# A two-layer DiT kernel on one core: which engine forms six of the 24 modulation units, and where in the program

## The chip, the core and the metric

The kernel runs on one core of a Trainium2 chip. Its engines run side by side, each in its own order: TensorE (PE; its weight loads are listed as PEld), VectorE (DVE), ScalarE (ACT), GpSimd (POOL), and SyncE (SP), which here issues DMAs. They wait for each other by semaphores. The metric is the device time of one execution in microseconds (us), the median of the runs taken; lower is better.

## The reference, cut to what matters

Two layers over 512 latent rows and 256 context rows, width 2048, in float32. Each layer first forms a modulation (shift, scale, gate) for both kinds of rows from two condition vectors:

```python
for i in range(DEPTH):                                  # DEPTH = 2
    shift, scale, gate       = split((silu(c)     @ ada_w[i] + ada_b[i])[:, None, :], 3)   # 2048 -> 3*2048
    shift_c, scale_c, gate_c = split( silu(c_ctx) @ ada_w[i] + ada_b[i], 3)
    h  = rmsnorm(x,  norm_w[i]) * (1 + scale)   + shift
    hc = rmsnorm(xc, norm_w[i]) * (1 + scale_c) + shift_c
    y, yc = even_mix(h, hc, ...) if i % 2 == 0 else odd_mix(h, hc, ...)   # both begin with h @ w_in, hc @ w_in
    x = x + gate * y
    if need_ctx: xc = xc + gate_c * yc                  # layer 0 only
return rmsnorm(x, final_norm)
```

`even_mix` (layer 0) is pooling and latent attention; `odd_mix` (layer 1) is a bidirectional mLSTM and windowed attention.

## The kernel before, in words

The modulation weights are two matrices of 2048 x 6144, together 24 **units** of 2048 x 512 (4 MB each). Units 0 to 7 are the shift and scale of layer 0, 8 to 11 its gate, 12 to 19 the shift and scale of layer 1, 20 to 23 its gate. A unit is needed for both condition vectors, except 20 to 23, which the context rows don't use: these are the **light** units here, the others the **heavy** ones. There are three ways to form a unit:

- `ada_steps` (L133), units 0 to 7 at the start: PE multiplies in float32, 16 matmuls of 32 columns of weights into the four quarters of one PSUM tile `pa`.
- `ada_pe_steps` (L154), units 18 and 19: the same, in four batches of four matmuls; DVE transposes the result (`gat`, L167), PE folds it (`pb`, L170) and DVE adds the bias (`av`, L131).
- `ada_vec_steps` (L174), the other 14 units: no PE. A step loads 256 KB of weights (`at`, L180, a DMA from SP into one of four buffers) and DVE multiplies it by a scalar and adds it to an accumulator (`acc`, L187): two such instructions in a heavy step, one in a light one. After 16 steps each accumulator is transposed and reduced (`atr`, `red`, L192 and L193: two more steps in a heavy unit, one in a light one), and one fold on PE (`pb`, L199) with four `av` on DVE ends the unit.

`Background` (L206) takes such steps one by one; `bg.step(n)` lets the surrounding code put n of them at a place.

The **in-projection** of layer 0 is 14 groups of 256 columns. Its groups 2 to 13 are `in_group` (L502): for each of four quarters `kq`, `load_w` (L111) loads 512 KB of weights (`wraw`, three buffers) and splits them in two **halves** into a rounded part (`wh`, a cast on ACT, L108) and a rest (`wl`, a subtraction on DVE, L109), four buffers each; then `tmode` (L301) multiplies: 24 pairs of a 512-row matmul into `px` (L309) and a 256-row one into `pc` (L311) per quarter. Groups 4 to 7 also do the pooling: `pool_mean` on DVE, then `pool_mix`, six short matmuls (`ppx`, L568) after quarters 1 and 3 of groups 5 and 7. Behind group 13 comes latent attention.

The **value products** of layer 1 are `mv_group` (L1199), heads 1 to 3: `kmode` (L314, matmuls at L322) with `load_w` in the same way, and between them `ctx_state` (L1215), which scales the context's values on DVE (`wv`, L1219), splits them (`wvh` on ACT, `wvl` on DVE) and multiplies them on PE (L1228). One more group of the same width follows (`odw[5]`, L1239).

PE's order in these stages, and all other engines', comes from a scheduler that places each instruction by its own estimate; so a step can stand some way off from where the code puts it. Each engine then works strictly in that order, and SP too: a `wraw` load behind an `at` load is not issued before it.

Of the kernel before, what the change touches and what calls it, by code (L numbers as in the profile page):

```python
# [8 lines left out]
F32 = mybir.dt.float32  # L9
# [7 lines left out]
P = 128  # L17
# [21 lines left out]
def tile_hybrid_dit(ctx: ExitStack, tc: tile.TileContext, ts: dict, out: bass.AP, dbg=None, upto=99):  # L39
    nc = tc.nc  # L40
    T, V, S, G, DM = nc.tensor, nc.vector, nc.scalar, nc.gpsimd, nc.sync

    def opool(es, name, side=None, bufs=1):
        return es.enter_context(tc.tile_pool(name=name, bufs=bufs, side=side, reuse_waits="tile"))
# [16 lines left out]
    def ppool(es, name, **bufs):  # L61
        return Banks(es, name, **bufs)
# [24 lines left out]
    st = cst.tile([P, KC, 32], F32, name="st")  # L87
# [12 lines left out]
    fold = con[:, C_FOLD : C_FOLD + 32]  # L100
# [24 lines left out]
    def ada_place(u, pb, n):  # L125

        a = cst.tile([P, 4, 2], F32, name=f"av{u}")
        for b4 in range(4):
            sl = slice(32 * b4, 32 * b4 + 32)
            ab = vec[sl, V_AB + 8 * u : V_AB + 8 * u + 8].rearrange("p (b v) -> p b v", v=2)  # L130
            V.tensor_tensor(a[sl, :, :n], pb[:, :n, b4::4].rearrange("p v b -> p b v"), ab[:, :, :n], op=ALU.add)  # L131
        av[u] = a

    def ada_steps(u, pp, tp, nb=3, nt=2):

        pa = pp.tile([P, 512], F32, name=f"pa{u}", tag="pm")
        for q in range(4):
            at = []
            for i in range(2):
                at.append(tp.tile([P, 2, 512], F32, name=f"at{u}_{q}_{i}", tag="ada", bufs=nb))  # L140
                DM.dma_start(at[i], ts["ada"][u, 2 * q + i].rearrange("p (k w) -> p k w", w=512))
            for qd in range(4):
                T.matmul(pa[32 * qd : 32 * qd + 32, :], st[:, 4 * q + qd, :], at[qd // 2][:, qd % 2, :],
                         start=q == 0, stop=q == 3, skip_group_check=True)
            if q == 3:
                tr = tp.tile([P, 16, 32], F32, name=f"ga{u}", tag="ga", bufs=1)
                V.transpose(tr.rearrange("p b r -> p (b r)"), pa)
                yield
                pb = pp.tile([32, 2, 16], F32, name=f"pb{u}", tag="pm")
                T.matmul(pb, fold, tr[:, :, 0:2].rearrange("p b v -> p v b"), start=True, stop=True)  # L150
                ada_place(u, pb, 2)
            yield

    def ada_pe_steps(u, pp, tp, nb):  # L154

        pa = pp.tile([P, 512], F32, name=f"pa{u}", tag="pm")
        for q in range(4):
            at = []
            for i in range(4):
                kc = 4 * q + i  # L160
                at.append(tp.tile([P, 512], F32, name=f"at{u}_{kc}", tag="ada", bufs=nb))
                DM.dma_start(at[i], ts["ada"][u, kc // 2][:, (kc % 2) * 512 : (kc % 2) * 512 + 512])
            for qd in range(4):
                T.matmul(pa[32 * qd : 32 * qd + 32, :], st[:, 4 * q + qd, :], at[qd], start=q == 0, stop=q == 3, skip_group_check=True)
            if q == 3:
                tr = ta("gat", 512).rearrange("p (b r) -> p b r", r=32)
                V.transpose(tr.rearrange("p b r -> p (b r)"), pa)  # L167
                yield
                pb = pp.tile([32, 2, 16], F32, name=f"pb{u}", tag="pm")
                T.matmul(pb, fold, tr[:, :, 0:2].rearrange("p b v -> p v b"), start=True, stop=True)  # L170
                ada_place(u, pb, 2)
            yield
# [183 lines left out]
    pp = ppool(esP, "ppA", px=4, pc=2, pm0=1, pm1=1)  # L356

    def new_px(n=1):
        return [pp.tile([P, 512], F32, name="px", tag="px", bufs=4) for _ in range(n)]

    def new_pc():
        return pp.tile([P, 2, 256], F32, name="pc", tag="pc", bufs=2)
# [94 lines left out]
    ap_ = opool(esA, "phA")  # L457
    OX, OC, NP = 8, 8 + NX + 8, 8 + NX + 8 + NC + 8

    def ta(name, n=NT):  # L460
        return ap_.tile([P, NP], F32, name=name, tag="ta", bufs=6)[:, :n]

    def c_evac(pairs, ssq):

        res = []
        for px, pc in pairs:
            r = ta("craw")
            S.copy(r[:, :NX], px)
            V.tensor_copy(r[:, NX:], pc)
            res.append(r)  # L470
        for r in res:
            sq = ta("csq") if ssq[1] else ssq[0]
            S.activation(sq, r, AF.Square)
            if ssq[1]:
                V.tensor_tensor(ssq[0], ssq[0], sq, op=ALU.add)
            ssq[1] += 1
        return res
# [12 lines left out]
    pc = new_pc()  # L490
# [9 lines left out]
    S.copy(kr[:, NX:], pc[:, 0, :])  # L500
    split(kr, KH, KL)

    bg = Background(range(8, 14), pp, ap_, 4, "ta", 6)

    def in_group(g, between=(), steps=(1, 1)):
        px, pc = new_px(2), new_pc()
        for kq in range(4):
            w = load_w(win[g, kq])
            bg.step(steps[0])
            tmode(px, [pc[:, b, :] for b in range(2)], w, range(4 * kq, 4 * kq + 4), HX0, HC0, kq == 0, kq == 3)  # L510
            bg.step(steps[1])
            if kq < len(between):
                between[kq]()
        return px, pc
# [2 lines left out]
    ssq = [ap_.tile([P, NT], F32, name="ssqc", tag="ssqc", bufs=1), 0]  # L517
    raw = []
    for g in range(2):
        px, pc = in_group(2 + g, steps=(2, 2))  # L520
        raw += c_evac([(px[b], pc[:, b, :]) for b in range(2)], ssq)
    p6 = pp.tile([P, 6], F32, name="cps6", tag="pm")
    stat_mm(p6, ssq[0], 6, 512)
# [46 lines left out]
        return z  # L570

    for pr in range(2):
        px, pc = in_group(4 + 2 * pr, steps=(1, 0))
        ds, zs = [], []

        def mean(b):
            ds.append(pool_mean(2 * pr + b, px[b], pc[:, b, :]))

        def mix(b):
            zs.append(pool_mix(2 * pr + b, ds[b]))  # L580

        mean(0)
        qx, qc = in_group(5 + 2 * pr, (lambda: mean(1), lambda: mix(0), lambda: None, lambda: mix(1)), (0, 0))
        for b in range(2):
            t = ta("psg")
            S.activation(t[:, :NX], qx[b], AF.Silu)
            S.activation(t[:, NX:], qc[:, b, :], AF.Silu)
            V.tensor_tensor(t, zs[b], t, op=ALU.mult)
            G.dma_start(zd[2 * pr + b], t)


    for i in range(6):
        if i < 2:
            pe = ada_pe_steps(18 + i, pp, ap_, 4)
            px, pc = in_group(8 + i, (lambda: next(pe), lambda: next(pe), lambda: next(pe), lambda: (next(pe), next(pe))), (0, 0))
        else:
            px, pc = in_group(8 + i, steps=(2, 2))
        for b in range(2):
            t = ta("sag")
            S.activation(t[:, :NX], px[b], AF.Silu)  # L600
            S.activation(t[:, NX:], pc[:, b, :], AF.Silu)
            G.dma_start(agd[2 * i + b], t)
# [7 lines left out]
    pp = ppool(esP, "ppM", s2=2, pj=2, pm=2)  # L610
# [19 lines left out]
    for j in range(4):  # L630
        r = tf("cqr")
# [276 lines left out]
    pp = ppool(esP, "ppO", px=4, pc=2, pm=2)  # L908
# [3 lines left out]
    bg = Background(range(14, 18), pp, tz, 4, "ht", 3)  # L912
# [66 lines left out]
    for i in range(2):  # L979
        for b, px in enumerate(x_group_t(G_MQ + i)):  # L980
            q = htp.tile([P, NX], F32, name="mqt", tag="mqt", bufs=2)
# [54 lines left out]
    for i in range(2):  # L1036
        px, pc = new_px(2), new_pc()
# [98 lines left out]
    for d in range(2):  # L1136
# [20 lines left out]
        tr = gs.tile([4, 4], F32, name="tr", tag="tr", bufs=2)  # L1157
# [34 lines left out]
    eg.close()  # L1192


    ea = ExitStack()
    bg = Background(range(20, 24), pp, opool(ea, "ada1"), 4, "atr", 1)


    def mv_group(h, state):  # L1199
        px, pc = new_px(2), new_pc()  # L1200
        pv = [px[b // 2][:, 256 * (b % 2) : 256 * (b % 2) + 256] for b in range(4)]
        for kq in range(4):
            w = load_w(odw[1 + h, kq])
            kcs = range(4 * kq, 4 * kq + 4)
            bg.step(2)
            kmode(pv, w, kcs, HX, kq == 0, kq == 3, 2)
            bg.step(3)
            kmode([pc[:, b, :] for b in range(2)], w, kcs, HC, kq == 0, kq == 3, 2)
            if kq % 2 == 0:
                next(state, None)  # L1210
        vx_store(h, [p_.rearrange("p (a b) -> p a b", b=256) for p_ in px])
        return vc_store([pc])
# [25 lines left out]
    px, pc = new_px(2), new_pc()  # L1238
    for kq in range(4):  # L1239
        w = load_w(odw[5, kq])  # L1240
        bg.step(2)
        tmode(px, [pc[:, b, :] for b in range(2)], w, range(4 * kq, 4 * kq + 4), HX, HC, kq == 0, kq == 3)
        if kq % 2 == 0:
            next(state, None)
    bg.finish()
    ea.close()
    for b in range(2):
        t = cm.tile([P, NX], F32, name="akx", tag="kxt", bufs=2)
        S.copy(t, px[b])
# [24 lines left out]
    pp = ppool(esP, "ppL", px=4, pm=4)  # L1274
# [168 lines left out]
    pp = ppool(esP, "ppW", px=2, s2=2, pm=1, po=1)  # L1443
# [303 lines left out]
    pp = ppool(esP, "ppF", px=4, pm=2)  # L1747
    for g in range(3, 7):
        px = new_px(2)
# [13 lines left out]
    for h in range(2):  # L1763
        sl = slice(256 * h, 256 * h + 256)
        px = [p_[:, :256] for p_ in new_px(2)]
# [138 lines left out]
```

## Time and profile before

| | |
|---|---|
| median of 3 runs | 2305.13 us (2303.32 to 2306.37) |
| the profiled execution, its own time | 2305.76 us |
| its span | 2304.0 us |
| PE, PEld busy | 2229.1 us (97%), 1894.9 us (82%) |
| DVE, ACT, POOL busy | 1406.7 us (61%), 916.3 us (40%), 162.8 us (7%) |
| in-projection groups 2 to 13 | about 164 to 589 us of the span |
| value products and the group behind them | about 1412 to 1570 us |

In the profile an instruction is named by line, engine, operation and tile, as `L187 DVE ... acc<-at,st,acc`. A matmul's listed duration overlaps with the next one's; the time that a matmul takes is read from the distance of two starts.

### The profile page before, as it was taken

How to read it: one execution, taken by the hardware profiler on the slowest of the kernel's cores; microseconds unless marked ns; L12 is line 12 of the kernel's file. 1: busy time of each engine (PE TensorE's matmuls, PEld its weight loads, DVE VectorE, ACT ScalarE, POOL GpSimd, SP SyncE). 2: the span in 40 equal slices, each digit the busy share in tenths (PEclk: the TensorE clock that was granted, in tenths of full speed). 3: DMA queues.
4: the chain of work that ended last, by engine and by line, in shares of the span. 5: the costliest groups of instructions: out<-in, count | busy, mean ns of one | idle time of the engine just before them, and what ended most of it. 6: DMA issues, size and time to landing. Idle time of an engine off the chain costs nothing. (4 is left out here: it accounts for less than half of the span.)

```text
span 2304.0 us, 34221 instructions
## 1 busy us (share of the span) xinstructions
PE 2229.1 (97%) x13000; PEld 1894.9 (82%) x13000; DVE 1406.7 (61%) x2841; ACT 916.3 (40%) x1864; POOL 162.8 (7%) x203
## 2 busy tenths in 40 slices
PE   5999999999999999999999999999999999999998
PEld 3678888788899999888888799988888878777887
DVE  5579523296666666788558524763455587778434
ACT  4232222112444444542226322223556667656432
POOL 0000100000000000011113100000000000003110
PEclk9999999999999999999999999999999999999999
DMA  9855323565211112276444321753232312113433
GB/s 386 322 202 179 121 85 115 185 227 186 100 49 54 51 56 69 101 252 224 160 158 154 93 100 65 247 185 120 88 101 94 103 61 68 65 55 122 135 113 116
DMA packets 118005, 309.14 MB, mean 134 GB/s; under 512 B 13612, under 2 KB 21292, under 8 KB 117840
## 3 DMA queue, kind: packets, MB, share of 16 engines
q1 hardware_dynamic: 110960, 279.64, 36.2%
q0 software_dynamic: 6880, 27.32, 3.2%
q8 instruction: 102, 1.67, 0.3%
q14 instruction: 63, 0.52, 0.1%
HBM read 277.28 MB, written 29.62 MB: 133 GB/s over the span
## 5 line engine op out<-in xcount | busy, mean ns | idle before, releaser
L108 ACT CAST wh<-wraw 128x512 fp32r<-128x512 f32 (+2 forms) x540 | 316.1, 590 | 852.5 <-PE pc L311 372.1
L109 DVE TENSOR_TENSOR wl<-wraw,wh 128x512 fp32r<-128x512 f32 (+2 forms) x540 | 358.5, 669 | 467.7 <-ACT wh L108 464.4
L187 DVE SCALAR_TENSOR_TENSOR acc<-at,st,acc 128x512 f32<-128x512 f32 x360 | 251.9, 749 | 25.8 <-DMA at<-in_ada_dram 24.2
L322 PE MATMUL px<-wh,hxh 128*128 128x512 f32 (+2 forms) x512 | 174.9, 342 | 0.8 <-ACT sz L1310 0.8
L322 PE MATMUL px<-wl,hxh 128*128 128x512 f32 (+2 forms) x512 | 174.0, 340 | 0.0
L322 PE MATMUL px<-wh,hxl 128*128 128x512 f32 (+2 forms) x512 | 173.9, 340 | 0.0
L309 PE MATMUL px<-h0h,wh 128*128 128x512 f32 x384 | 152.9, 398 | 0.0
L309 PE MATMUL px<-h0h,wl 128*128 128x512 f32 x384 | 151.7, 395 | 0.3 <-DVE wl L109 0.3
L309 PE MATMUL px<-h0l,wh 128*128 128x512 f32 x384 | 151.6, 395 | 0.0
L311 PE MATMUL pc<-h0h,wl 128*128 128x256 f32 x400 | 112.7, 282 | 0.0
L311 PE MATMUL pc<-h0h,wh 128*128 128x256 f32 x400 | 112.5, 281 | 0.0
L311 PE MATMUL pc<-h0l,wh 128*128 128x256 f32 x400 | 112.4, 281 | 0.0
L322 PEld LDWEIGHTS px<-wh,hxh 128*128 128x128 f32 x512 | 96.7, 189 | 13.6 <-ACT sz L1310 1.9
L322 PEld LDWEIGHTS px<-wl,hxh 128*128 128x128 f32 x512 | 96.7, 189 | 11.2
L322 PEld LDWEIGHTS px<-wh,hxl 128*128 128x128 f32 x512 | 96.6, 189 | 11.2
L309 PEld LDWEIGHTS px<-h0h,wh 128*128 128x128 f32 x384 | 72.1, 188 | 22.9 <-ACT wh L108 4.2
L309 PE MATMUL px<-hxh,wh 128*128 128x512 f32 x224 | 89.7, 400 | 0.0
L309 PE MATMUL px<-zxl,wh 128*128 128x512 f32 x224 | 89.3, 399 | 0.0
L309 PE MATMUL px<-hxl,wh 128*128 128x512 f32 x224 | 89.2, 398 | 0.0
L309 PE MATMUL px<-hxh,wl 128*128 128x512 f32 x224 | 89.1, 398 | 0.0
L309 PE MATMUL px<-zxh,wl 128*128 128x512 f32 x224 | 88.7, 396 | 0.0
L309 PE MATMUL px<-zxh,wh 128*128 128x512 f32 x224 | 88.2, 394 | 0.0
(887 smaller groups left out, 6010.1 us busy)
## 6 DMA issues: line engine op xcount, KB each, us to landing
at<-in_ada_dram SPq DMA_DIRECT2D x256, 256.0 KB, 3.4
at<-in_ada_dram SPq DMA_DIRECT2D x64, 512.0 KB, 7.9
wraw<-in_od_in_dram SPq DMA_DIRECT2D x64, 512.0 KB, 3.5
wraw<-in_ev_in_dram SPq DMA_DIRECT2D x56, 512.0 KB, 4.2
wraw<-in_ev_out_dram SPq DMA_DIRECT2D x44, 512.0 KB, 3.9
wraw<-in_od_oz_dram SPq DMA_DIRECT2D x32, 512.0 KB, 3.5
wraw<-in_od_out_dram SPq DMA_DIRECT2D x32, 512.0 KB, 3.5
xt<-in_xT_dram SPq DMA_DIRECT2D x16, 384.0 KB, 7.3
```

The source lines that it names most:

```text
L108: S.copy(h, src)
L109: low.tensor_tensor(l, src, h, op=ALU.subtract)
L187: V.scalar_tensor_tensor(a, at, st[:, kc, v : v + 1], a, op0=ALU.mult, op1=ALU.add)
L309: T.matmul(px[b], w_, Hx[kc][r_], start=s0, stop=s1)
L311: T.matmul(pc[b], w_, Hc[kc][r_], start=s0 and b == 0, stop=s1, skip_group_check=True)
L322: T.matmul(p_, h_, w_, start=s0, stop=s1, skip_group_check=True)
```

## The change

Units 18 and 19 leave PE, and `ada_pe_steps` is removed; units 20 to 23 leave the value products; all six become steps of `ada_vec_steps` under the in-projection. Its list of units grows from six to twelve: 8, 9, then the light 20 to 23, then 10 to 13, 18 and 19. The steps per quarter change from 2+2, 1+0, 0+0 and 2+2 in groups 2-3, 4 and 6, 5 and 7 to 9, and 10-13, to 2+1 in groups 2-3, 2+2 in groups 4 to 7, and 3+2 in groups 8 to 13.

```diff
-    def ada_pe_steps(u, pp, tp, nb):
...
-    bg = Background(range(8, 14), pp, ap_, 4, "ta", 6)
+    bg = Background((8, 9, 20, 21, 22, 23, 10, 11, 12, 13, 18, 19), pp, ap_, 4, "ta", 6)
...
-        px, pc = in_group(2 + g, steps=(2, 2))
+        px, pc = in_group(2 + g, steps=(2, 1))
...
-        px, pc = in_group(4 + 2 * pr, steps=(1, 0))
+        px, pc = in_group(4 + 2 * pr, steps=(2, 2))
...
-        qx, qc = in_group(5 + 2 * pr, (lambda: mean(1), lambda: mix(0), lambda: None, lambda: mix(1)), (0, 0))
+        qx, qc = in_group(5 + 2 * pr, (lambda: mean(1), lambda: mix(0), lambda: None, lambda: mix(1)), (2, 2))
...
     for i in range(6):
-        if i < 2:
-            pe = ada_pe_steps(18 + i, pp, ap_, 4)
-            px, pc = in_group(8 + i, (lambda: next(pe), lambda: next(pe), lambda: next(pe), lambda: (next(pe), next(pe))), (0, 0))
-        else:
-            px, pc = in_group(8 + i, steps=(2, 2))
+        px, pc = in_group(8 + i, steps=(3, 2))
...
-    ea = ExitStack()
-    bg = Background(range(20, 24), pp, opool(ea, "ada1"), 4, "atr", 1)
...
-            bg.step(2)
             kmode(pv, w, kcs, HX, kq == 0, kq == 3, 2)
-            bg.step(3)
             kmode([pc[:, b, :] for b in range(2)], w, kcs, HC, kq == 0, kq == 3, 2)
...
-        bg.step(2)
         tmode(px, [pc[:, b, :] for b in range(2)], w, range(4 * kq, 4 * kq + 4), HX, HC, kq == 0, kq == 3)
...
-    bg.finish()
-    ea.close()
```

On PE, at the end of quarter 0 of group 8, the first batch of unit 18 stands between two pairs before:

```order
L309 MATMUL px<-h0h_167,wl 128x512
L311 MATMUL pc<-h0h_167,wl 128x256
L164 MATMUL pa_3408<-at_0_3409,st 32x512
L164 MATMUL pa_3408<-at_1_3411,st 32x512
L164 MATMUL pa_3408<-at_2_3413,st 32x512
L164 MATMUL pa_3408<-at_3_3415,st 32x512
L309 MATMUL px<-h0h_169,wh 128x512
L311 MATMUL pc<-h0h_169,wh 128x256
```

There are eight such batches in groups 8 and 9; now the pairs follow each other without them, and in groups 8 to 13 only six folds of two short matmuls (`pb<-red`) stand between pairs.

On DVE, groups 8 and 9 before (L588 is the end of the pooling, `gat` and `av` belong to units 18 and 19, `acc` in the last row to unit 10):

```order
L588 TENSOR_TENSOR psg<-pz,psg 128x768 x2
L109 TENSOR_TENSOR wl<-wraw,wh 128x512 x8
L167 STREAM_TRANSPOSE gat<-pa_3408 128x512
L131 TENSOR_TENSOR av_3635<-pb_3633,vec 32x8 x4
L109 TENSOR_TENSOR wl<-wraw,wh 128x512 x8
L167 STREAM_TRANSPOSE gat<-pa_3709 128x512
L131 TENSOR_TENSOR av_3936<-pb_3934,vec 32x8 x4
L187 SCALAR_TENSOR_TENSOR acc_0_2788<-at_4_3962,st,acc_0_2788 128x512
```

and in the changed program a stretch of the same groups (L167 is now the line of the accumulation, here of unit 10):

```order
L109 TENSOR_TENSOR wl<-wraw,wh 128x512
L167 SCALAR_TENSOR_TENSOR acc_0_3756<-at_4_3843,st,acc_0_3756 128x512
L167 SCALAR_TENSOR_TENSOR acc_1_3757<-at_5_3847,st,acc_1_3757 128x512
L167 SCALAR_TENSOR_TENSOR acc_0_3756<-at_5_3847,st,acc_0_3756 128x512
L167 SCALAR_TENSOR_TENSOR acc_1_3757<-at_6_3851,st,acc_1_3757 128x512
L167 SCALAR_TENSOR_TENSOR acc_0_3756<-at_6_3851,st,acc_0_3756 128x512
L109 TENSOR_TENSOR wl<-wraw,wh 128x512
```

Where a half's split `wl` stood next to the next one, five or six accumulations stand between them now; this goes on to the end of group 13.

On DVE in the value products, around the scaling `wv` of head 2's context state before (`acc` is unit 22):

```order
L187 SCALAR_TENSOR_TENSOR acc_0_15034<-at_5_15141,st,acc_0_15034 128x512
L109 TENSOR_TENSOR wl<-wraw,wh 128x512
L187 SCALAR_TENSOR_TENSOR acc_0_15034<-at_6_15196,st,acc_0_15034 128x512
L187 SCALAR_TENSOR_TENSOR acc_0_15034<-at_7_15199,st,acc_0_15034 128x512
L1219 TENSOR_SCALAR wv<-vcx,wcol 128x258 x2
L187 SCALAR_TENSOR_TENSOR acc_0_15034<-at_8_15250,st,acc_0_15034 128x512
L109 TENSOR_TENSOR wl<-wraw,wh 128x512
L109 TENSOR_TENSOR wvl<-wv,wvh 128x516
```

and now, for the same head (`wv` is L1190, `c0l` the rest of the state formed before):

```order
L109 TENSOR_TENSOR wl<-wraw,wh 128x512 x4
L109 TENSOR_TENSOR c0l_13447<-pc_15226,c0h_13446 128x258
L109 TENSOR_TENSOR wl<-wraw,wh 128x512
L1190 TENSOR_SCALAR wv<-vcx,wcol 128x258 x2
L109 TENSOR_TENSOR wl<-wraw,wh 128x512
L109 TENSOR_TENSOR wvl<-wv,wvh 128x516
```

No accumulation, and so no wait for an `at` load, stands ahead of `wv` any more. Outside these two stages the order of every engine is as before.

## Rows read from the trace of the kernel before

**Rows 1.** Waits of PE, whole span: total us, times, longest.
```profile
PE ps L267 <- DVE rb L395: 23.0, 1, 23.0
...
PE pc L1228 <- ACT wvh L108: 3.9, 1, 3.9
...
PE px L309 <- DVE wl L109: 0.3, 1, 0.3
```
**Rows 2.** Timeline of PE in group 8: start, us, instruction.
```profile
384.86 0.39 PE L309 MATMUL px<-h0h,wl 128*128 128x512 f32 x1
...
385.29 1.07 PE L164 MATMUL pa<-at,st 128*32 128x512 f32 x8
386.29 0.50 PE L309 MATMUL px<-h0h,wh 128*128 128x512 f32 x1
...
386.75 0.40 PE L309 MATMUL px<-h0l,wh 128*128 128x512 f32 x1
```
**Rows 3.** The same: quarters 24 pairs apart, starts of groups 8, 10, last pair, fold.
```profile
254.47 0.40 PE L309 MATMUL px<-h0h,wh 128*128 128x512 f32 x1
...
262.95 0.40 PE L309 MATMUL px<-h0h,wh 128*128 128x512 f32 x1
...
376.74 0.39 PE L309 MATMUL px<-h0h,wh 128*128 128x512 f32 x1
...
479.17 0.39 PE L309 MATMUL px<-h0h,wl 128*128 128x512 f32 x1
...
479.79 0.50 PE L309 MATMUL px<-h0h,wh 128*128 128x512 f32 x1
...
496.54 0.39 PE L309 MATMUL px<-h0h,wh 128*128 128x512 f32 x1
...
504.86 0.39 PE L309 MATMUL px<-h0h,wh 128*128 128x512 f32 x1
...
588.47 0.39 PE L309 MATMUL px<-h0h,wl 128*128 128x512 f32 x1
```
**Rows 4.** Stretches: us, busy us per engine (x), PE's granted clock, DMA share, GB/s.
```profile
1480.00:1490.00 10.00, 10.00 (x88) 10.00 (x87) 6.72 (x14) 3.42 (x6) 0.54 (x1) 1.00 0.76 253
1490.00:1500.00 10.00, 8.97 (x77) 8.77 (x76) 5.47 (x9) 1.10 (x2) 0.00 (x0) 1.00 0.71 237
1500.00:1510.00 10.00, 6.26 (x38) 6.06 (x39) 8.18 (x16) 2.66 (x5) 0.00 (x0) 0.83 0.87 283
```
**Rows 5.** Timeline of all engines there: start, us, instruction, idle before it.
```profile
1498.09 1.54 DVE L187 SCALAR_TENSOR_TENSOR acc<-at,st,acc 128x512 f32<-128x512 f32 x2 [3.83 <-DMA at<-in_ada_dram]
...
1501.59 0.61 DVE L1219 TENSOR_SCALAR wv<-vcx,wcol 128x258 f32<-128x258 f32 x2
...
1502.91 0.38 PE L1228 MATMUL pc<-wvh,mkch 128*128 128x258 f32 x1 [3.94 <-ACT wvh L108]
```
**Rows 6.** Timeline of DVE in groups 10 and 11.
```profile
464.62 5.39 DVE L187 SCALAR_TENSOR_TENSOR acc<-at,st,acc 128x512 f32<-128x512 f32 x8 [1.76 <-DMA at<-in_ada_dram]
469.93 1.29 DVE L109 TENSOR_TENSOR wl<-wraw,wh 128x512 fp32r<-128x512 f32 x2
471.13 5.39 DVE L187 SCALAR_TENSOR_TENSOR acc<-at,st,acc 128x512 f32<-128x512 f32 x8
...
477.64 1.30 DVE L192 STREAM_TRANSPOSE atr<-acc 128x512 f32<-128x512 f32 x2
478.86 1.24 DVE L193 TENSOR_REDUCE red<-atr 128x16 f32<-128x512 f32 x2
480.01 0.48 DVE L182 TENSOR_SCALAR acc<-at,st 128x512 f32<-128x512 f32 x1
```
**Rows 7.** Timeline of DVE later in group 12.
```profile
539.02 0.69 DVE L109 TENSOR_TENSOR wl<-wraw,wh 128x512 fp32r<-128x512 f32 x1 [3.47 <-ACT wh L108]
```
**Rows 8.** DVE by line, 164 to 589 us: busy us, mean ns, idle before.
```profile
L187 DVE SCALAR_TENSOR_TENSOR acc<-at,st,acc 128x512 f32<-128x512 f32 x174 | 118.6, 744 | 4.3 <-DMA at<-in_ada_dram 4.1
```
**Rows 9.** The same, 1412 to 1570 us.
```profile
L187 DVE SCALAR_TENSOR_TENSOR acc<-at,st,acc 128x512 f32<-128x512 f32 x60 | 44.9, 749 | 18.5 <-DMA at<-in_ada_dram 17.2 <-DVE acc L187 0.3
```

More of the change, by code (lines that the diff above doesn't have):

```diff
@@ L146, in ada_steps @@
                 tr = tp.tile([P, 16, 32], F32, name=f"ga{u}", tag="ga", bufs=1)
[L147 to L152, printed above, removed]
-    def ada_pe_steps(u, pp, tp, nb):
[L156 to L166, printed above, removed]
                 V.transpose(tr.rearrange("p b r -> p (b r)"), pa)
```

## The prediction

> **What bounds the kernel now.** I read the page first: PE is busy 97% of the span, so a change pays only if it takes work or a wait off PE. Then the waits of PE [rows 1]: the largest, 23.0 us, lies at the start and is not touched; of the two stages that are, the value products have one wait of 3.9 us for `wvh`, and the whole in-projection has 0.3 us. So the in-projection is bound by PE's own work, which the timeline measures [rows 2, 3], and the value products lose time at one place, which the stretches and the timeline of all engines show [rows 4, 5]. The reader is to see in rows 2 that a batch of `pa` pushes two pairs apart, in rows 4 that two stretches hold fewer matmuls than the one before. The question is then whether DVE can carry six more units under the in-projection without making PE wait; that is read from DVE's timeline and its groups by line [rows 6 to 9].
>
> **In-projection, PE.** A pair normally starts 0.35 us after the one before. Around a batch of four `pa` matmuls the distance is 386.29 - 384.86 = 1.43 us, and the next pair takes 0.46 us [rows 2]; so a batch costs 1.43 + 0.46 - 2 x 0.35 = 1.19 us, and the eight that go cost 9.5 us.
>
> Not all of that need come back, because pairs run at two paces: 24 of them, a quarter, took 8.48 us at 254 us and 8.32 us at 497 us [rows 3], with PE waiting for nothing at either place. Groups 8 to 13 took from 376.74 to 588.47 + 0.35, 212.1 us. In the changed order they hold 24 quarters and six folds. A fold costs 0.62 - 0.35 = 0.27 us in its own distance (479.17 to 479.79) and, by the pair behind the batch, 0.11 us more: 0.38 us. At the slow pace that is 24 x 8.48 + 6 x 0.38 = 205.8 us, a gain of 6.3 us; at the fast pace 202.0 us, a gain of 10.1 us. I take the slow one: group 8 is entered slow before, and the pace changed there only behind longer interruptions (pooling, `pa`), which groups 8 to 13 no longer have, while the fold at 479 left a fast pace fast. Both ends stay in the range.
>
> Folds elsewhere: groups 2 to 7 get five instead of one (units 8, 9, 20, 21, 22), 1.5 us more; the value products and the group behind them lose the four of units 20 to 23, for which I use the same price, 1.5 us less. They cancel.
>
> **Value products.** Stretches of 10 us hold 88 matmuls, then 77, then 38 [rows 4]: 61 are missing, at 10 / 88 = 0.114 us each 6.9 us. [...] The cause stands in rows 5: DVE sat 3.83 us before an accumulation until its `at` load had come, `wv` was queued behind that accumulation and started at 1501.59, and PE's matmul followed at 1502.91. With no accumulation ahead of `wv` the stall goes with its slow clock: 6.9 us. What is late next there: `wv` waits for ACT's copy of the values at a group's end, and PE wants `wvh` a quarter later, 72 matmuls or 8.2 us, while `wv` to the matmul took 1.3 us. So nothing takes its place; the lower bound is no gain, if ACT's copy or cast is the late one.
>
> **In-projection, DVE: what the six units cost and what hides them.** Eight accumulations took 5.31 us (464.62 to 469.93), 0.664 us each; two splits 1.20 us; two transposes 1.22 us, two reductions 1.15 us; a first product is 0.48 us [rows 6]. With four bias adds, bounded by a reduction (0.6 us), a heavy unit is 30 x 0.664 + 0.5 + 1.2 + 1.2 + 0.6 = 23.4 us in 18 steps, 1.30 us a step. At five steps a quarter in groups 9 to 13, DVE needs 6.5 + 1.2 = 7.7 us against PE's 8.3 to 8.5 us: 92%, dense but enough. In groups 4 to 7 a light step is one accumulation, and the pooling has room.
>
> The cover is the lead. A half may be split as soon as PE leaves the fourth half before it; at 539.02 a split had waited 3.47 us for just that [rows 7], so DVE was ahead by nearly three halves, 3 x 4.2 us less a cast and a split, about 11 us. And with eight accumulations between splits [rows 6], denser than the five or six now, PE waited only 0.3 us in the stage. If the cover went, each us that DVE is behind a quarter would be a us of PE in each of 20 quarters.
>
> The loads: four buffers reach four steps ahead. For heavy steps that is 8 x 0.664 = 5.3 us, and in the in-projection 174 accumulations (87 loads) waited 4.1 us, 0.05 us a load [rows 8]. For light steps it is 2.7 us, and 60 accumulations waited 17.2 us, 0.29 us each [rows 9]. So units 20 to 23 bring such waits into groups 4 to 8: four steps and two splits are 4 x (0.664 + 0.29) + 1.2 = 5.0 us of a quarter's 8.48. Volume: five loads of 256 KB and one of 512 KB in 8.48 us are about 216 GB/s, while one stretch moved 283 GB/s [rows 4]. Free, then, with this end kept: if heavy loads also waited 0.29 us, a quarter would be 7.7 + 1.45 = 9.15 us, PE would fall behind by 20 x (9.15 - 8.48) - 11 = 2.4 us.
>
> [...]
>
> **Sum.** 6.3 + 6.9 = 13.2 us off. The profiled execution took 2305.76 us (span 2304.0), 0.03% from the median, so the median moves alike: 2305.1 - 13.2 = 2292 us.
>
> **Rivals.**
> 1. *The fast pace*: groups 8 to 13 at 8.32 us a quarter give 10.1 + 6.9 = 17.0 us, 2288 us. For it: the late groups run fast before. Against: what turned them fast is taken out.
> 2. *DVE is just too slow, or the stall in the value products only shrinks*: waits of 0.29 us a heavy load, or a late cast there. The gain is then 13.2 less 2.4 to 6.9 us: 2294 to 2299 us. For it: light loads did wait so long. Against: rows 8, and the short chain of rows 5.
> 3. *The loads pace DVE, and DVE paces PE; slower*. SP issues in order, so a weight load stands behind loads that wait for DVE, and a late load delays the split behind it, the next load's buffer, and the weights. With w us of waiting a load, PE loses 20 x (7.7 + 5w - 8.48) - 11 us. That eats the 13.2 us at w = 0.40; at w = 0.5 it is 23 us, 2315 us, and each pause of PE adds a slow clock as in rows 4. For it: the 0.29 us of rows 9 and the 216 GB/s of loads, all through one queue. Against: 0.05 us in rows 8.
> 4. *Nothing measurable*: w about 0.35, or a new stall at the change to attention, where DVE carries four leftover steps (as before, but from a shorter lead): 2301 to 2309 us.
>
> **Chances.** Main 0.48, rival 1 0.25, rival 2 0.14, rival 4 0.08, rival 3 0.05. The range from 2285 to 2300 us holds the first three, with 3 us below rival 1 for both terms' error. What this kernel's measurement can tell from no change is about 0.2%, 4.6 us; below 2300.5 us counts as faster: 0.48 + 0.25 + 0.14 = 0.87, within 0.08, slower 0.05.
>
> **What would show it.** In the changed profile: no `pa` after 150 us, and groups 8 to 13 in 202 to 206 us; a quarter of 8.48 or 8.32 us settles the pace. DVE's splits there still waiting for ACT now and then, as in rows 7; PE's wait for `wl` under 1 us. In the value products no wait for `wvh`, every 10 us stretch at 86 to 88 matmuls and a clock of 1.00. I am wrong if `px` waits for `wl` by several us, if `acc` waits for `at` by over 0.3 us a load in groups 9 to 13, or if the wait for `wvh` stays.

## The result, and the profile after

| | before | after |
|---|---|---|
| median | 2305.81 us, 6 runs (2303.32 to 2309.93) | 2293.77 us, 6 runs (2288.86 to 2296.03) |
| ratio | | 0.9942, 95% interval 0.9927 to 0.9957 |
| profiled execution, span | 2305.76, 2304.0 us | 2295.59, 2293.8 us |
| DVE busy | 1406.7 us (61%) | 1452.3 us (63%) |

The kernel became 12.0 us faster; 13.2 us were forecast (2292 us, range 2285 to 2300). Where the profiled executions part is read from when PE reaches the same instruction in each:

| PE reaches | before | after | difference, us |
|---|---|---|---|
| the first `gkr` matmul, early in the in-projection | 50.25 | 52.04 | +1.8 |
| group 8, first pair | 376.74 | 379.04 | +2.3 |
| group 13, last pair | 588.47 | 584.34 | -4.1 |
| `pc<-wvh`, the last ahead of the old stall | 1481.28 | 1477.39 | -3.9 |
| `pc<-wvh`, the first behind its slow clock | 1523.58 | 1512.46 | -11.1 |
| `pc<-wvh`, the last of the stage | 1558.70 | 1547.41 | -11.3 |
| `bc`, in the next stage | 1575.60 | 1565.30 | -10.3 |

Groups 8 to 13 gained 6.4 us and the stretch with the stall 7.2 us, both where the prediction put them. Of the 7.2 us, 0.4 belong to a fold (`pb`) of a light unit that stood there before:

```profile
1511.80 0.28 PE L322 MATMUL px<-wh,hxl 128*128 128x256 f32 x1
1512.01 0.23 PE L199 MATMUL pb<-red,con 128*32 128x16 f32 x2
1512.17 0.38 PE L322 MATMUL pc<-wh,hch 128*128 128x256 f32 x1
1512.39 0.28 PE L322 MATMUL pc<-wl,hch 128*128 128x256 f32 x1
```

The matmuls around it take 1512.39 - 1511.80 = 0.59 us where two take 0.23 elsewhere. So the stall itself gave back 6.8 us.

The 1.8 us at the start are hardly from the change. The stretch from 45 to 50 us shows what they are; its columns are those of [rows 4], with all engines. Before:

```profile
45.00:50.00 5.00, 5.00 (x27) 3.40 (x27) 0.67 (x2) 0.07 (x1) 0.00 (x0) 0.85 1.02 411
```

After:

```profile
45.00:50.00 5.00, 5.00 (x19) 2.61 (x18) 1.02 (x2) 0.42 (x1) 0.00 (x0) 0.50 1.02 410
```

Behind the same early pause of 2.15 us PE runs at a granted clock of 0.50 for the whole 5 us in this execution; in the other it is 0.50 up to 46.5 us and 1.00 from 47 us on. In the profiles of the experiments, which share this opening, the same instruction comes from 1.5 us earlier to 1.8 us later than before; it is 1.4 us later in one that leaves the kernel before as it was up to there (heavy_only_six) and 0.3 us later in one that has the whole change (toggle). A single profile can be off by that much. The one of the changed kernel lies 1.8 us above the median of its runs, the one before at its median, which fits the 12.0 us of the medians against the 10.2 us of the spans.

The timeline of PE after, which answers to [rows 2, 3]: the first pairs of two quarters of group 8, the pair ahead of a fold and the one behind it, and the last pair of group 13.

```profile
379.04 0.39 PE L289 MATMUL px<-h0h,wh 128*128 128x512 f32 x1
...
387.51 0.40 PE L289 MATMUL px<-h0h,wh 128*128 128x512 f32 x1
...
404.12 0.39 PE L289 MATMUL px<-h0h,wl 128*128 128x512 f32 x1
...
404.72 0.50 PE L289 MATMUL px<-h0h,wh 128*128 128x512 f32 x1
...
584.34 0.39 PE L289 MATMUL px<-h0h,wl 128*128 128x512 f32 x1
```

A quarter takes 387.51 - 379.04 = 8.47 us, the slow pace, and a fold 0.60 us between pairs. The six groups take 584.34 + 0.35 - 379.04 = 205.65 us; forecast were 205.8 us.

The three stretches with the same times as in [rows 4]:

```profile
1480.00:1490.00 10.00, 10.00 (x88) 10.00 (x87) 3.08 (x7) 3.53 (x6) 0.54 (x1) 1.00 0.33 112
1490.00:1500.00 10.00, 10.00 (x88) 10.00 (x87) 2.48 (x5) 2.14 (x4) 0.00 (x0) 1.00 0.29 97
1500.00:1510.00 10.00, 10.00 (x88) 10.00 (x87) 1.39 (x2) 1.24 (x2) 0.00 (x0) 1.00 0.17 54
```

88 matmuls in each, clock 1.00: no pause and no slow clock behind it. Before, the clock was 0.50 from about 1504 to 1507 us, behind the pause, and 1.00 from 1508 us on. Of PE's waits, those of the value products and the steps behind them, 1412 to 1600 us (total us, times, longest), this is the only one:

```profile
PE bc L1304 <- ACT selh L1256: 1.1, 1, 1.1
```

It wasn't there before, and in this profile about 1 us of what the stage gave back (-11.3 to -10.3 in the table) is lost again at the next hand-over. ACT had itself waited 1.1 us for a load (`selr`) that was issued 6.3 us earlier; before, 4.5 us lay between the two and nobody waited. In light_only, toggle and double_mix below, which have lost the stall too, PE doesn't wait there. So this wait is not shown to be a price of the change.

DVE under the in-projection, answering to [rows 6, 7]: one stretch at the end of group 9, one in group 12.

```profile
443.83 0.69 DVE L109 TENSOR_TENSOR wl<-wraw,wh 128x512 fp32r<-128x512 f32 x1 [2.15 <-ACT wh L108]
448.07 0.69 DVE L109 TENSOR_TENSOR wl<-wraw,wh 128x512 fp32r<-128x512 f32 x1 [3.55 <-ACT wh L108]
...
526.54 3.40 DVE L167 SCALAR_TENSOR_TENSOR acc<-at,st,acc 128x512 f32<-128x512 f32 x5
529.85 0.68 DVE L109 TENSOR_TENSOR wl<-wraw,wh 128x512 fp32r<-128x512 f32 x1
530.46 3.39 DVE L167 SCALAR_TENSOR_TENSOR acc<-at,st,acc 128x512 f32<-128x512 f32 x5
534.01 0.69 DVE L109 TENSOR_TENSOR wl<-wraw,wh 128x512 fp32r<-128x512 f32 x1 [0.16 <-ACT wh L108]
```

DVE still waits now and then for the buffers that PE has to leave (3.55 us, and 0.16 in the densest part, behind casts of ACT of which those at 443 and 533 us had themselves waited 3.6 us for PE), so its lead is full again there; five accumulations cost 529.85 - 526.54 = 3.31 us, 0.662 each. Its groups by line over groups 8 to 13 (379 to 585 us), answering to [rows 8], and over groups 4 to 7 (246 to 379 us):

```profile
L167 DVE SCALAR_TENSOR_TENSOR acc<-at,st,acc 128x512 f32<-128x512 f32 x183 | 125.4, 743 | 3.8 <-DMA at<-in_ada_dram 3.4
...
L167 DVE SCALAR_TENSOR_TENSOR acc<-at,st,acc 128x512 f32<-128x512 f32 x58 | 43.6, 751 | 18.2 <-DMA at<-in_ada_dram 16.9
```

The light units took their waits along, 16.9 / 58 = 0.29 us a load, as in the value products [rows 9]; the heavy ones waited 3.4 us over 183 accumulations. In neither place did PE notice: it waits for no `wl` in groups 2 to 13.

### The profile page after: what moved, and what is told of

Same layout as the page of the kernel before. It is cut to its first block, busy times and chain, and to the rows that moved or that the text cites. A ratio compares the mean times of both kernels' runs of the same rounds, so it can differ in the third digit from the quotient of the medians.

```text
span 2293.8 us, 34183 instructions
## 1 busy us (share of the span) xinstructions
PE 2220.6 (97%) x12936; PEld 1892.2 (82%) x12936; DVE 1452.3 (63%) x2909; ACT 918.4 (40%) x1866; POOL 163.8 (7%) x203
## 5 line engine op out<-in xcount | busy, mean ns | idle before, releaser
L167 DVE SCALAR_TENSOR_TENSOR acc<-at,st,acc 128x512 f32<-128x512 f32 x420 | 294.1, 749 | 24.6 <-DMA at<-in_ada_dram 22.9
L289 PEld LDWEIGHTS px<-h0h,wl 128*128 128x128 f32 x384 | 72.1, 188 | 17.6
```

The lines of the kernel that those rows point to most:

```text
L167: V.scalar_tensor_tensor(a, at, st[:, kc, v : v + 1], a, op0=ALU.mult, op1=ALU.add)
L289: T.matmul(px[b], w_, Hx[kc][r_], start=s0, stop=s1)
```

## The experiments

Each is compared with the kernel before, run beside it on the same chip. The changed kernel was not run beside them: where one is set against it, about 1 us stays open, since the kernel before has medians from 2304.63 to 2305.81 us in the sets.

**The light units alone.** The changed kernel's list without 18 and 19; these stay on PE as before.

```diff
-    bg = Background(range(8, 14), pp, ap_, 4, "ta", 6)
+    bg = Background((8, 9, 20, 21, 22, 23, 10, 11, 12, 13), pp, ap_, 4, "ta", 6)
...
-        px, pc = in_group(4 + 2 * pr, steps=(1, 0))
+        px, pc = in_group(4 + 2 * pr, steps=(2, 2))
...
-            px, pc = in_group(8 + i, steps=(2, 2))
+            px, pc = in_group(8 + i, steps=(3, 2))
```

(Groups 5 and 7 get 2+2 steps too, and the value products lose theirs, as in the change.)

> Only the light units 20 to 23 move under the in-projection (2+2 steps in groups 2 to 7, 3+2 in groups 10 to 13); units 18 and 19 stay on PE in groups 8 and 9. Theory, two separate gains: the value products lose their stall (7.1 us between the two traces), groups 8 to 13 keep their 212 us, and the folds in groups 2 to 7 cost about 0.5 us: 2305.8 - 7.1 + 0.5 = about 2299 us, no wait for wvh. Rival, one gain that needs both parts (the units on PE also kept DVE's order or PE's pace from what the changed kernel has): either no gain beyond 2 us, or nearly the whole 12 us.

2299.67 us, ratio 0.9977 (0.9967 to 0.9988). PE's waits hold no `wvh`; groups 8 to 13 took 591.39 + 0.35 - 378.64 = 213.1 us, 1 us over before.

**The heavy units alone.**

```diff
-    bg = Background(range(8, 14), pp, ap_, 4, "ta", 6)
+    bg = Background((8, 9, 10, 11, 12, 13, 18, 19), pp, ap_, 4, "ta", 6)
...
-        px, pc = in_group(4 + 2 * pr, steps=(1, 0))
+        px, pc = in_group(4 + 2 * pr, steps=(2, 0))
...
-        if i < 2:
-            pe = ada_pe_steps(18 + i, pp, ap_, 4)
...
+        px, pc = in_group(8 + i, steps=(2, 2))
```

> Only units 18 and 19 leave PE, to DVE under the in-projection (2+2 steps in groups 8 to 13, 2+0 in groups 4 and 6); units 20 to 23 stay in the value products. Theory, two separate gains: groups 8 to 13 fall from 212 us to 205.6 us at the slow pace of 8.48 us a quarter, the wait for wvh stays near 3.9 us: 2305.8 - 6.5 = about 2299 us. Should groups 8 to 13 run at 8.32 us a quarter, 2295 us. Rival: the gain of groups 8 to 13 is not the pa batches but comes with the lighter DVE queue elsewhere: then less than 3 us.

2299.14 us, ratio 0.9970 (0.9957 to 0.9982). Groups 8 to 13 took 581.16 + 0.35 - 375.84 = 205.7 us, and the wait in the value products is still there (PE's waits):

```profile
PE pc L1224 <- ACT wvh L108: 3.1, 1, 3.1
```

The two parts gain 5.4 and 6.0 us, 11.4 together, and both at once 12.0: they are separate, each in its own stage, as the sum had them.

**Six buffers in the value products.** What late thing made the stall?

```diff
-    bg = Background(range(20, 24), pp, opool(ea, "ada1"), 4, "atr", 1)
+    bg = Background(range(20, 24), pp, opool(ea, "ada1"), 6, "atr", 1)
```

> The kernel before, with six at buffers instead of four for the units in the value products; nothing else. Theory A, the stall there comes from loads that are issued too late (four buffers reach only 2.7 us ahead, a load takes 3.4 to 3.6 us): with six, 4 us ahead, DVE's 17 us of waiting for at shrink to under 6 us and the wait for wvh to under 1 us: about 2299 us. Theory B, the load is held behind a weight load or by the sharing of the DMA engines, whatever its buffer: the wait for wvh stays at 3 to 4 us, 2304 to 2306 us.

2300.13 us, ratio 0.9972 (0.9961 to 0.9984). Theory A. PE's waits in the value products, DVE by line from 1412 to 1570 us, and the stretch that had held 38 matmuls:

```profile
PE pc L1228 <- DVE wvl L109: 0.4, 1, 0.4
```

```profile
L187 DVE SCALAR_TENSOR_TENSOR acc<-at,st,acc 128x512 f32<-128x512 f32 x60 | 45.0, 749 | 5.7 <-DMA at<-in_ada_dram 4.4
```

```profile
1500.00:1510.00 10.00, 10.00 (x87) 9.84 (x86) 9.72 (x16) 1.25 (x2) 0.00 (x0) 1.00 0.91 287
```

The wait for `wvh` is gone, 17.2 us of waiting for loads [rows 9] became 4.4, and the 38 matmuls 87, with all 60 accumulations still in place and DVE busy 97% of that stretch. So DVE was not too full there; its loads were asked for too late.

**Both at once, the other way.** Units 18 and 19 to DVE, six buffers in the value products, the light units left where they were: the two edits above, joined.

> Units 18 and 19 leave PE for DVE, units 20 to 23 stay in the value products with six at buffers there. Theory, the two gains add and the stall needs only the earlier loads: 2305 - 6 (as with the heavy units alone) - 5 to 7 (as with six buffers alone) = 2292 to 2294 us, level with the changed kernel. Rival, moving the light units gives something that earlier loads do not: 2296 us or more, with a wait of PE for wvh or wvl left over 1 us.

2293.56 us, ratio 0.9947 (0.9934 to 0.9960): level with the changed kernel.

```profile
PE pc L1224 <- DVE wvl L109: 0.8, 1, 0.8
...
PE pc L1224 <- ACT wvh L108: 0.3, 1, 0.3
```

PE still waits these 1.1 us there, but moving the light units gives nothing on top that can be measured.

**Two buffers under the in-projection.** Is the cover that the prediction named the real one?

```diff
-    bg = Background((8, 9, 20, 21, 22, 23, 10, 11, 12, 13, 18, 19), pp, ap_, 4, "ta", 6)
+    bg = Background((8, 9, 20, 21, 22, 23, 10, 11, 12, 13, 18, 19), pp, ap_, 2, "ta", 6)
```

> The changed kernel with two at buffers instead of four under the in-projection. Theory, four buffers are what hides the loads: two reach two heavy steps ahead, 2 x 1.33 = 2.7 us, under the 3.4 us to landing and the issue; each heavy load waits 0.5 to 0.75 us, and the formula of the third rival, 20 x (7.7 + 5w - 8.48) - 11, gives 23 to 48 us: 2317 to 2342 us, with px or pc waiting for wl. Rival, the loads are not near the limit: DVE waits more for at, but PE loses less than 3 us, 2297 us at most.

2348.31 us, ratio 1.0190 (1.0174 to 1.0205): 54 us slower than the changed kernel, over the range. DVE from 379 to 600 us, then PE's waits from 164 to 700 us (in part), and the first pair of group 8 and the last of group 13:

```profile
L167 DVE SCALAR_TENSOR_TENSOR acc<-at,st,acc 128x512 f32<-128x512 f32 x162 | 114.5, 748 | 57.1 <-DMA at<-in_ada_dram 56.2
```

```profile
PE pj L642 <- DVE av L131: 14.2, 1, 14.2
PE pj L642 <- DVE vl L109: 8.7, 1, 8.7
PE px L289 <- DVE wl L109: 8.4, 7, 1.9
PE cps L247 <- DVE ssqc L455: 5.5, 1, 5.5
```

```profile
391.73 0.39 PE L289 MATMUL px<-h0h,wh 128*128 128x512 f32 x1
...
612.55 0.40 PE L289 MATMUL px<-h0h,wl 128*128 128x512 f32 x1
```

81 loads waited 56.2 us, 0.69 each; the formula gives 20 x (7.7 + 3.5 - 8.48) - 11 = 43 us. The last pair of group 13 comes 612.55 - 584.34 = 28 us later. But group 8 already starts 391.73 - 379.04 = 12.7 us later: ahead of it PE waits 5.5 us for `ssqc`, a sum of squares that DVE reaches late among its accumulations, and has a clock of 0.50 from 245 to 250 us. Groups 8 to 13 themselves lose 15.5 us. Then the attention stands 14.2 us and 8.7 us, because DVE has steps left over, and PE's clock is 0.67 from 620 to 640 us. From group 8 on the loss is some 42 us (54 less 12.7), near the formula's 43; but most of it is paid in the attention, where DVE settles what it still owes, and the 12.7 us ahead of the dense groups are not in the formula.

**Denser steps.** How much room was left?

```diff
-        px, pc = in_group(8 + i, steps=(3, 2))
+        px, pc = in_group(8 + i, steps=(4, 3))
```

> The changed kernel with 4+3 steps a quarter in groups 8 to 13 instead of 3+2, so the same units are formed in fewer quarters. Theory, DVE's room is 8.48 us a quarter and its lead 11 us: seven heavy steps and two splits are 7 x 1.30 + 1.2 = 10.3 us, 1.8 us too many in each of some 15 quarters with heavy steps, 28 us less the 11 us of lead: PE loses about 17 us, 2311 us, with px or pc waiting for wl from group 10 or 11 on. Rival, the lead or the room is larger than worked out: no wait for wl, 2294 us.

2311.31 us, ratio 1.0028 (1.0017 to 1.0039), 17.5 us above the changed kernel where 17 were expected (18.7 us if each is set against its own kernel before). PE's waits from 377 to 610 us, and two stretches:

```profile
PE px L289 <- DVE wl L109: 13.1, 7, 3.6
```

```profile
460.00:480.00 20.00, 18.23 (x96) 15.58 (x97) 19.59 (x35) 3.21 (x5) 0.00 (x0) 0.91 0.62 200
480.00:500.00 20.00, 16.96 (x80) 14.15 (x79) 19.93 (x36) 4.13 (x8) 1.08 (x2) 0.83 0.75 247
```

The first wait for `wl` comes at 461 us, in group 10. The waits are 13.1 us; the rest of the loss goes with the clock at 0.83 and 0.91 behind them. DVE is now busy 98 to 100%: this is what the stage looks like when it, and no longer PE, sets the pace.

**The pace, three tries.** Why a quarter takes 8.48 or 8.32 us decides between the forecast and its first rival. First try: the second mixing of each pair is put off by two quarters.

```diff
-        qx, qc = in_group(5 + 2 * pr, (lambda: mean(1), lambda: mix(0), lambda: None, lambda: mix(1)), (2, 2))
+        qx, qc = in_group(5 + 2 * pr, (lambda: mean(1), lambda: mix(0)), (2, 2))
...
-        px, pc = in_group(8 + i, steps=(3, 2))
+        px, pc = in_group(8 + i, (lambda: None, late) if i == 0 else (), (3, 2))
```

(`late` is that mixing with its gate; group 6 takes it in the same way for the first pair.)

> The changed kernel, but the second mixing of each pooling pair (six matmuls ppx) stands after quarter 1 of the next group and not after quarter 3 of its own. In both traces the pace is fast (8.32 us a quarter) behind each interruption that stands after quarter 1, and slow (8.48) behind those after quarters 0, 2 and 3. Theory, the place of the last long interruption sets the pace: with none left after quarter 3, all from the middle of group 5 to the end of group 13 runs fast, 30 more quarters than now, 30 x 0.16 = 4.8 us less: about 2289 us, groups 8 to 13 in 201 to 203 us with the mixing in group 8 (1.1 us). Rival, the pace comes by chance or from what stands before it: groups 8 to 13 stay at 8.48 us a quarter, time as the changed kernel within 1 us.

2295.82 us, ratio 0.9955 (0.9943 to 0.9967). PE's timeline, two pairs 24 apart ahead of the moved mixing in group 6 and two behind it:

```profile
304.55 0.39 PE L289 MATMUL px<-h0h,wh 128*128 128x512 f32 x1
...
312.87 0.39 PE L289 MATMUL px<-h0h,wh 128*128 128x512 f32 x1
...
339.11 0.40 PE L289 MATMUL px<-h0h,wl 128*128 128x512 f32 x1
...
347.59 0.40 PE L289 MATMUL px<-h0h,wl 128*128 128x512 f32 x1
```

8.32 us ahead, 8.48 behind: a mixing after quarter 1 turned the pace slow, and groups 9 to 13 ran slow. The place is not it. (The 2 us more than the changed kernel go with the mixing in group 7, which now waits 1.6 us for `wpoolh`; the pairs behind it start 0.58 and 0.64 us apart instead of 0.35, at 362.75, 363.33 and 363.97 us.) Each mixing so far had turned the pace over, save that one behind a wait, so the second try counts matmuls:

```diff
+        if g == 3:
+            qx = pp.tile([P, 512], F32, name="ppd", tag="pm")
+            for n in range(6):
+                T.matmul(qx[:, :64], wpool, d[0][:, OX : OX + 64], start=n == 0, stop=n == 5)
```

> The changed kernel with six more short matmuls (64 columns, into a PSUM tile that nobody reads) two pairs into group 8, some 0.4 us of PE. In the traces so far each mixing (six matmuls) turned the pace over: slow to fast or fast to slow, after quarter 1 and after quarter 3, save one that lay behind a wait. Theory, six matmuls between pairs turn the pace over, however short: groups 8 to 13 turn from 8.48 to 8.32 us a quarter, 24 x 0.16 - 0.4 = 3.4 us less than the changed kernel, about 2290 us. Rival, what turns the pace is the length of the pause or the place: groups 8 to 13 stay at 8.48 us a quarter and the time is 2294 us or 0.4 us over.

2293.96 us, ratio 0.9956 (0.9942 to 0.9969). Inconclusive: the six waited 3.3 us for a free PSUM tile, and the theory has no pause in it. Slow behind that, the pace turned fast at the next fold, at 410 us. The third try has no wait:

```diff
+            if g % 2 and nn < 512:
+                for n in range(6):
+                    T.matmul(qx[:, nn : nn + 64], w_, r_[:, sl.start : sl.start + 64], start=n == 0, stop=n == 5, skip_group_check=True)
```

> The changed kernel, with six more short matmuls (64 columns, into a part of the same PSUM tile that nobody reads) directly behind the mixing at the end of groups 5 and 7, so that nothing waits, unlike in the run with six matmuls in group 8. About 0.3 us of PE each. Theory, each six matmuls turn the pace over: twelve turn it twice, the pace stays fast from the middle of group 5 to the end of group 13, 30 x 0.16 - 0.6 = 4.2 us less than the changed kernel, about 2289.6 us. Rival, the pace does not follow the count: groups 6 and 8 to 13 at 8.48 us a quarter or of mixed paces, 2293 to 2295 us.

2292.11 us (2291.49 to 2293.72), ratio 0.9943 (0.9931 to 0.9955). Pairs 24 apart behind the doubled mixing of group 7, and behind the first fold after it:

```profile
389.77 0.40 PE L289 MATMUL px<-h0h,wl 128*128 128x512 f32 x1
...
398.25 0.40 PE L289 MATMUL px<-h0h,wl 128*128 128x512 f32 x1
...
410.53 0.39 PE L289 MATMUL px<-h0h,wh 128*128 128x512 f32 x1
...
418.85 0.39 PE L289 MATMUL px<-h0h,wh 128*128 128x512 f32 x1
```

Slow behind the twelve, against the theory; then the fold at 405 us turned it fast, and it stayed so to the end of group 13, though the same fold left it slow in the changed kernel. The count is not it either. Groups 8 to 13 took 581.59 + 0.35 - 379.46 = 202.5 us, close to the first rival's 202.0. This version is the lowest median of all, but its interval doesn't part it from the changed kernel.

## Why the prediction was right

- *PE's batches*: 6.3 us forecast, 6.4 measured; alone, 6.0 by the medians. That all of the 9.5 us don't come back, since the late groups lose their fast pace, came out as written. The argument for the slow pace was weaker than the result: a fold does not always leave the pace as it is (double_mix), and no run names what sets it. That the slow pace came was in part luck; the fast one, which the range allowed for, would have brought 3.8 us more.
- *The stall*: 6.9 us forecast, 6.8 measured in the timeline without the fold; 5.4 us by the medians for the light units alone, folds included. Its cause was put rightly on the `at` load; six_buffers shows it. In the stage nothing took its place; behind it `bc` waits 1.1 us in the profile after, and not in others that have lost the stall.
- *Folds*: 1.5 us more in groups 2 to 7 were forecast, for five folds instead of one. PE has four there (at 255, 299, 334 and 369 us), so three more, 1.1 us; it came 0.5 us later over these groups, since the one wait for `wl` of before [rows 1], which cost 0.6 us at 184 us with what followed it, is gone as well. In the value products PE gained 0.4 us at each of two of the four folds (at 1478 and 1512 us before). Both signs held, and the terms were too small to matter.
- *DVE's room and lead*: 92% of a quarter, 0.664 us an accumulation, 11 us of lead. The denser kernel was worked out from these three and met within 2 us. Under the in-projection the accumulations again start closer together than they last by their listing, 0.662 us apart with 743 ns listed.
- *The loads*: 0.29 us a light load was forecast to come along and to stay hidden, and did. The third rival was right about the mechanism, and wrong about this kernel: it needs w = 0.40, the heavy loads had 3.4 us in 183 accumulations. With two buffers it is what happens, at 0.69 us a load. That each pause of PE adds a slow clock does not hold in the profile after: behind the 1.1 us ahead of `bc` the clock stays at 1.00.
- *What is left open*: what sets the pace. Three rules (place, count, folds keep it) fell. Most interruptions turned it in the same way in kernel after kernel, but none of the runs names the cause.

## What to carry to other kernels

Moving work off the bound engine pays what the bound engine's own timeline says, not the sum of the removed durations: measure the distance around the removed piece and the pace of the stretch without it. Before work is moved away from a wait, look whether its loads are only issued too late: two more buffers were worth as much here (5.0 us) as moving four units (5.4 us). In this kernel, the engine that feeds the bound one was free up to its room in the narrowest stretch plus its lead; the room was read from the distances of its starts, the lead from a place where it waits. What it still owed at the end of the stage was paid in the next (14.2 and 8.7 us of waiting in two_buffers).

## Not expected of the hardware

The same 24 pairs take 8.32 or 8.48 us on PE at a granted clock of 1.00 with no wait, and keep to one of the two over whole groups until something stands between two pairs. Over the 24 quarters of groups 8 to 13 this is 3.8 us, a third of what the change gained.
